# Product keys with 112 candidate sums a head, one-hot comparisons of four tokens, gates moved to the first keys' rows, and offset rows loaded ahead

## The chip, the cores and the metric

The kernel runs on one NeuronCore of one Trainium2 chip. The metric is device time in microseconds, the median of several runs. The engines are named as in the profile: PE (TensorE, matrix products), DVE (VectorE), ACT (ScalarE), POOL (GpSimd) and SP (the queue that issues the weight loads).

## The reference

Two blocks follow each other over 256 tokens of width 1024. The change touches the first block, and one preparation for the second.

First block: a mixer (`h @ w_in`, two branches with sigmoid gates `zg`, two branch products `ab`, `w_out`), then the retrieval of experts by product keys:

```
s = einsum('thpc,hpkc->thpk', q, sub_keys)          # 8 heads, 2 halves, 128 keys
top_s, top_i = top_k(s, 16)
cand_s = top_s[:, :, 0, :, None] + top_s[:, :, 1, None, :]   # 16 x 16 = 256 sums a head
fin_s, fin_pos = top_k(cand_s, 16)
idx = cand_i at fin_pos                             # first key * 128 + second key
gates = softmax(fin_s)
act = gelu(u[idx] . h);  out = sum(gates * act * v[idx])
```

Second block: RWKV and MoBA mixing, then 32 experts with top 4; their weights are the large stream at the end, and their biases ("offsets", `moe_b`) are prepared in the first block.

## The kernel before

Products run in fp32r, in three matrix products for one: each 512-column piece of a weight is cut into a high part (ACT, line 282) and a low part (DVE, line 285; with `cut["aid"]` set, every fourth low part goes to POOL). `gemm` takes one piece for four groups of three 128x256 products (lines 215 to 217) and then calls `tick`, which hands out background work from the list `bg`: each entry has a cost, and `tick` emits entries while a credit (`rate` a tick) lasts. Nothing else sets the order; each engine runs its instructions in the order in which they were written. Weights come as 1 MB tiles through a ring that SP fills when a tile is free.

The stages that matter here, in order:

- `zg`: 8 units of two products each, followed by a sigmoid on ACT into `sg`.
- `ab`: 16 products of 12 matmuls. After products 0, 3 and 6 stands `offset_rows(i)`: a load of 512 columns of `moe_b` into `bf` by POOL's queue (line 501), a copy to `br` on ACT (line 502), two subtractions on POOL (line 504) and a store of `br` to `bd` (line 505). `bf` and `br` have one buffer each.
- `xo`, `qp`: the output product and the queries, with 32 searches for the first 16 of 128 keys (`topk16`, lines 579 to 584) as background work.
- Top-k stage, under the products `up` of the experts' first matrices (64 units of 48 matmuls): for each half of the tokens `cand` on POOL (line 602, four instructions of 128x512, 256 sums a head), eight searches over 256 sums, `place` (the two key positions from the place of a sum: a shift by 4, an AND with 15), `cmp` (comparison with 0 to 15 on DVE, line 646, and a product on POOL, line 649) and `red`.
- Gate stage, under the rest of `up`: for each token a 128x128 one-hot `ah` of the first key on POOL (line 752) and `bh` of the second key times the gate on DVE (line 753), a product `gp` of the two for four tokens (line 764), and `gate_put`, which multiplies the gates into the units that are done and copies them to the others. The loop over `up` leaves the top-k stage at the first unit after `bg` is empty; `credit["rate"]` then spreads the gate work over the units left.
- `vo`, RWKV and MoBA, and the 32 experts (`w<-in_moe_dram`).

Of the kernel before, what the change touches and what calls it, by code (L numbers as in the profile page):

```python
# [35 lines left out]
def tile_model(ctx: ExitStack, tc: tile.TileContext, a, out, taps=None):  # L36
    nc = tc.nc
# [72 lines left out]
    bd = dram.tile([128, 1536], F32R, name="bd")  # L110
# [7 lines left out]
    idx_t = p2.tile([128, 3, T], F32, name="idx_t")  # L118
    iota = p2.tile([128, 128], F32, name="iota")
# [23 lines left out]
    def part(x, k):  # L143
        return x[0][:, k, :], x[1][:, k, :]
# [243 lines left out]
    with ExitStack() as ph:  # L388
# [70 lines left out]
        for j in range(4):  # L459
            zc = psa.tile([128, 2, T], F32, tag="mm", name="zc")  # L460
            zv = psa.tile([128, T], F32, tag="mm", name="zv")
            z_chunk(zc[:, 0, :])
            z_chunk(zc[:, 1, :])
            csb = p1w.tile([128, 2, T], F32, tag="csb", name="csb")
            nc.scalar.copy(csb, zc)
            z_chunk(zv)
            u = p1w.tile([128, 2 + T], F32, tag="cu", name="cu")
            acc = p1w.tile([128, T], F32, tag="cacc", name="cacc")

            def conv_a(j=j, u=u, acc=acc, csb=csb, zv=zv):  # L470
# [12 lines left out]
            later(0.7, split, part(yT, j), acc)  # L483
        sg = p1.tile([128, 2, 8, T], F32, tag="sg", name="sg")
        for b in range(2):
            for m2 in range(4):
# [8 lines left out]
        bsp = ph.enter_context(tc.tile_pool(name="bsp", bufs=1))  # L495

        def offset_rows(i):

            f = bsp.tile([128, 512], F32, tag="bf", name="bf")
            r = bsp.tile([128, 512], F32R, tag="br", name="br")  # L500
            nc.gpsimd.dma_start(f, a["moe_b"][:, i * 512:(i + 1) * 512])
            nc.scalar.copy(r, f)
            for q in (slice(32, 64), slice(96, 128)):
                nc.gpsimd.tensor_tensor(r[q, :], f[q, :], r[q, :].bitcast(F32), op=ALU.subtract)
            nc.gpsimd.dma_start(bd[:, i * 512:(i + 1) * 512], r)

        mT = p1.tile([128, 8, T], F32, name="mT")
        for b, src in ((0, pT), (1, yT)):
            for m in range(8):
                ab = psa.tile([128, T], F32, tag="mm", name="ab")  # L510
                gemm(ab, src, 4, tick)
                if b == 0:
                    nc.vector.tensor_tensor(mT[:, m, :], sg[:, 0, m, :], ab, op=ALU.mult)
                else:
                    t2 = p1w.tile([128, T], F32, tag="t2", name="t2")
                    nc.vector.tensor_tensor(t2, sg[:, 1, m, :], ab, op=ALU.mult)
                    nc.gpsimd.tensor_tensor(mT[:, m, :], mT[:, m, :], t2, op=ALU.add)
                if b == 0 and m in (0, 3, 6):
                    offset_rows(m // 3)

        def m_of(k):
            split(part(hT, k), mT[:, k, :])
# [70 lines left out]
    def topk_of(t):  # L593
        ts, ti = ts2[t], ti2[t]
        tv = ts.rearrange("p (h s) k -> p h s k", s=2)
        big = {}

        def cand(i):
            if i == 0:
                big["c"] = tkw.tile([128, 8, 16, 16], F32, tag="big", name="cand")  # L600
            hh = slice(2 * i, 2 * i + 2)
            nc.gpsimd.tensor_tensor(big["c"][:, hh], tv[:, hh, 0, :, None].to_broadcast([128, 2, 16, 16]),
                                    tv[:, hh, 1, None, :].to_broadcast([128, 2, 16, 16]), op=ALU.add)
        for i in range(2):
            later(0.2, cand, i)
        fs = tkw.tile([128, 8, 16], F32, tag="fs", name="fs")
        fp = tkw.tile([128, 8, 16], U32, tag="fp", name="fp")
        for h in range(8):
            def one(h=h):
                topk16(big["c"][:, h].rearrange("p a b -> p (a b)"), fs[:, h], fp[:, h], 256, "r2")()  # L610
            bg.append((1.8, one))
            if h in (1, 3):
                later(0.2, cand, 2 + h // 2)
        sel = tkw.tile([128, 3, 128], F32, tag="sel", name="sel")

        e = tkw.tile([128, 8, 16], F32, tag="e", name="e")
# [10 lines left out]
                                    sm[:, :, None].to_broadcast([128, 8, 16]), op=ALU.mult)  # L627
        for s in range(2):
            def place(s=s):
                kq = tkw.tile([128, 8, 16], U32, tag="kq", name="kq")  # L630
                if s == 0:
                    nc.vector.tensor_scalar(kq, fp, 4, None, op0=ALU.logical_shift_right)
                else:
                    nc.vector.tensor_scalar(kq, fp, 15, None, op0=ALU.bitwise_and)
                kf = tkw.tile([128, 8, 16], F32, tag="kf", name="kf")
                nc.vector.tensor_copy(kf, kq)
                tf = tkw.tile([128, 8, 16], F32, tag="tf", name="tf")
                nc.vector.tensor_copy(tf, ti.rearrange("p (h s) k -> p h s k", s=2)[:, :, s, :])
                big["k"], big["t"] = kf, tf

            def cmp(i, s=s):
# [5 lines left out]
                                        big["k"][:, hh].rearrange("p h k -> p (h k)")[:, :, None].to_broadcast([128, 32, 16]),  # L647
                                        iota16[:, None, :].to_broadcast([128, 32, 16]), op=ALU.is_equal)
                nc.gpsimd.tensor_tensor(b, b, big["t"][:, hh, None, :].to_broadcast([128, 2, 16, 16]), op=ALU.mult)
            later(0.5, place)  # L650
            for i in range(4):
                later(0.65, cmp, i)

# [90 lines left out]
    hot = {}  # L744

    def one_hot(t0):

        ah = gw_p.tile([128, 2, 128], F32, tag="ah", name="ah", bufs=4)
        bh = gw_p.tile([128, 2, 128], F32, tag="bh", name="bh", bufs=4)
        for i in range(2):  # L750
            t = t0 + i
            nc.gpsimd.tensor_scalar(ah[:, i, :], iota, idx_t[:, 0, t:t + 1], None, op0=ALU.is_equal)  # L752
            nc.vector.tensor_scalar(bh[:, i, :], iota, idx_t[:, 1, t:t + 1], idx_t[:, 2, t:t + 1],
                                    op0=ALU.is_equal, op1=ALU.mult)
        hot[t0] = (ah, bh)

    gps = {}

    def gate_mm(t0):

        gp = psb.tile([128, 4, 128], F32, tag=f"acc{(t0 // 4) % 4}", name="gp")
        for i in range(4):
            ah, bh = hot[t0 + i - i % 2]
            nc.tensor.matmul(gp[:, i, :], ah[:, i % 2, :], bh[:, i % 2, :], start=True, stop=True)  # L764
        gps[t0] = gp

    def gate_put(t0):
# [1314 lines left out]
```

## Time and profile before

| what | before |
|---|---|
| median of 3 runs | 2248.0 us (2244.45 to 2250.05) |
| profiled execution, its own time | 2248.25 us |
| its span in the trace | 2246.4 us |
| PE busy | 2126.2 us, 95% |
| DVE busy | 1185.4 us, 53% |
| ACT busy | 742.3 us, 33% |
| POOL busy | 406.5 us, 18% |

The profiled execution lies 0.25 us above the median, and 1.85 us of it lie outside the span. The busy shares are means over stages: DVE is nearly always busy in the top-k stage and idle most of the time among the 32 experts. "Busy" of PE is modelled from pipelined instructions, so the number of matmuls in a stretch (x in brackets) tells more than the share.

### The profile page before, as it was taken

What the parts mean: (1) busy time and instruction counts of PE and PEld (TensorE: products, weight loads), DVE (VectorE), ACT (ScalarE), POOL (GpSimd) and SP (SyncE); (2) the same over time, 40 slices, a digit from 0 to 9 for tenths busy, and PEclk for the clock granted to TensorE, in tenths of its full rate; (3) what the DMA queues carried; (4) which work ended last, traced back from release to release, by engine and by line L of the source; (5) the groups of instructions that cost most, each with busy time, mean ns of one, the idle gap of its engine ahead of it and who ended that gap; (6) DMA issues with size and microseconds to landing.
All of it is one profiled execution on the core that took longest, in us unless ns stands there. A gap on an engine that the chain in (4) does not pass through costs nothing.

```text
span 2246.4 us, 34028 instructions
## 1 busy us (share of the span) xinstructions
PE 2126.2 (95%) x13130; PEld 1455.9 (65%) x13131; DVE 1185.4 (53%) x2527; ACT 742.3 (33%) x1591; POOL 406.5 (18%) x501
## 2 busy tenths in 40 slices
PE   8989998999999999999999989999999999999897
PEld 8979998999997788887878644333333333333332
DVE  5567998778888888867775522222222122221121
ACT  5545545444435555556553311110000000000000
POOL 3032365766650000001451100000000000000000
PEclk9999999999999999999998989999999999999999
DMA  5555444443336777765321689999999999999998
GB/s 214 191 174 188 170 153 155 144 137 146 132 132 235 288 282 281 284 220 189 119 95 40 256 344 408 420 420 419 420 419 420 420 419 420 419 419 420 420 420 315
DMA packets 90679, 627.07 MB, mean 279 GB/s; under 512 B 10248, under 2 KB 10960, under 8 KB 15760
## 3 DMA queue, kind: packets, MB, share of 16 engines
q1 hardware_dynamic: 88080, 616.68, 69.7%
q0 software_dynamic: 1664, 4.94, 0.6%
q10 hardware_dynamic: 768, 3.21, 0.4%
q8 instruction: 106, 1.74, 0.3%
q14 instruction: 61, 0.50, 0.1%
HBM read 621.86 MB, written 2.93 MB: 278 GB/s over the span
## 4 chain that ended last, share of the span: by engine, by line
PE 52%; DMA 36%; DVE 6%; issue 2%; ACT 2%; POOL 1%; SPq 0%; DVEq 0%; ACTq 0%; POOLq 0%
DMA w<-in_moe_dram 33%; PE vo L215 5%; PE vo L216 5%; PE vo L217 5%; PE up L217 4%; PE up L216 4%; PE up L215 4%; PE pdn L1862 2%; PE gp L764 2%; DVE ws L285 2%; DMA wm<-in_moe_dram 2%; PE pgate L1862 2%; PE pup L1862 2%; PE pgt L1787 1%; PE qp L215 1%
## 5 line engine op out<-in xcount | busy, mean ns | idle before, releaser
L285 DVE TENSOR_TENSOR ws<-w,ws 128x512 fp32r<-128x512 f32 x559 | 402.9, 726 | 148.2 <-ACT ws L282 140.3
L282 ACT CAST ws<-w 128x512 fp32r<-128x512 f32 x581 | 355.5, 623 | 184.3 <-PE vo L217 76.3
L1862 PE MATMUL pup<-w,xe 128*64 128x512 f32 x976 | 246.4, 595 | 30.1 <-DMA w<-in_moe_dram 29.9
L1862 PE MATMUL pgate<-w,xe 128*64 128x512 f32 x968 | 239.4, 597 | 14.1 <-DMA w<-in_moe_dram 13.6
L1862 PE MATMUL pdn<-w,at 128*64 128x512 f32 x968 | 227.2, 596 | 0.3 <-ACT at L1831 0.3
L217 PE MATMUL up<-h2h,ws 128*128 128x256 f32 x676 | 195.5, 289 | 10.3 <-POOL ws L285 6.6
L752 POOL TENSOR_SCALAR ah<-iota,idx_t 128x128 f32<-128x128 f32 x256 | 186.1, 743 | 95.7 <-PE gp L764 95.7
L215 PE MATMUL up<-h2h,ws 128*128 128x256 f32 x676 | 197.1, 292 | 1.7 <-ACT ws L282 1.7
L1862 PEld LDWEIGHTS pup<-w,xe 128*64 128x64 f32 x976 | 76.4, 137 | 186.3 <-issue 125.8
L216 PE MATMUL up<-h2l,ws 128*128 128x256 f32 x676 | 191.9, 284 | 0.0
L215 PE MATMUL vo<-ws,xh 128*128 128x512 f32 x480 | 189.0, 394 | 0.0
L216 PE MATMUL vo<-ws,xh 128*128 128x512 f32 x480 | 188.4, 393 | 0.6 <-DVE ws L285 0.6
L217 PE MATMUL vo<-ws,xl 128*128 128x512 f32 x480 | 187.7, 391 | 0.0
L1862 PEld LDWEIGHTS pgate<-w,xe 128*64 128x64 f32 x968 | 72.3, 137 | 148.8 <-issue 115.0
L1831 ACT COPY at<-pat 128x512 f32<-128x512 f32 x32 | 18.8, 587 | 452.6 <-PE pat L1830 452.6
L1862 PEld LDWEIGHTS pdn<-w,at 128*64 128x64 f32 x968 | 70.6, 137 | 125.4 <-issue 124.0
L1823 DVE TENSOR_SCALAR wm<-pup 128x512 f32<-128x512 f32 x32 | 22.1, 692 | 244.1 <-PE pup L1862 244.1
L1915 DVE TENSOR_TENSOR y<-pdn,gate 128x512 f32<-128x512 f32 (+1 forms) x33 | 22.2, 675 | 229.5 <-PE pdn L1862 229.5
L217 PEld LDWEIGHTS up<-h2h,ws 128*128 128x128 f32 x676 | 130.2, 193 | 15.7 <-DVE ws L285 8.1
L215 PEld LDWEIGHTS up<-h2h,ws 128*128 128x128 f32 x676 | 130.2, 193 | 2.4 <-ACT ws L282 2.3
L216 PEld LDWEIGHTS up<-h2l,ws 128*128 128x128 f32 x676 | 130.4, 193 | 0.0
L1822 ACT ACTIVATE wm<-act 128x512 f32<-128x512 f32 x32 | 20.2, 631 | 333.1 <-DVE act L1821 333.1
(684 smaller groups left out, 4220.4 us busy)
## 6 DMA issues: line engine op xcount, KB each, us to landing
w<-in_moe_dram SPq DMA_DIRECT2D x360, 1024.0 KB, 19.9
w<-in_eu_dram SPq DMA_DIRECT2D x64, 1024.0 KB, 4.8
w<-in_ev_dram SPq DMA_DIRECT2D x64, 1024.0 KB, 5.0
w<-in_w_ada_dram SPq DMA_DIRECT2D x24, 1024.0 KB, 5.5
wm<-in_moe_dram SPq DMA_DIRECT2D x20, 1024.0 KB, 19.9
w<-in_w_mix_dram SPq DMA_DIRECT2D x18, 1024.0 KB, 4.7
w<-in_w_in_dram SPq DMA_DIRECT2D x15, 1024.0 KB, 4.9
w<-in_w_q_dram SPq DMA_DIRECT2D x8, 1024.0 KB, 4.8
```

The lines of the kernel that those rows point to most:

```text
L215: nc.tensor.matmul(dst, lhs[0], rhs[0], start=start, stop=False)
L216: nc.tensor.matmul(dst, lhs[0], rhs[1], start=False, stop=False)
L217: nc.tensor.matmul(dst, lhs[1], rhs[0], start=False, stop=stop)
L282: nc.scalar.copy(h, src)
L285: eng.tensor_tensor(l, src, h.bitcast(F32), op=ALU.subtract)
L752: nc.gpsimd.tensor_scalar(ah[:, i, :], iota, idx_t[:, 0, t:t + 1], None, op0=ALU.is_equal)
L764: nc.tensor.matmul(gp[:, i, :], ah[:, i % 2, :], bh[:, i % 2, :], start=True, stop=True)
L1787: nc.tensor.matmul(p[:, k, :], x_sb[:, t, s], oh[:, t, :], start=(t == 0), stop=(t == 1))
L1822: nc.scalar.activation(sg, act, AF.Sigmoid, scale=1.702)
L1823: nc.vector.tensor_scalar(u, pu, 7.0, -7.0, op0=ALU.min, op1=ALU.max)
L1862: nc.tensor.matmul(p[hs[j], :], lhs[:, 4 * kh + k, hs[j]], g[j][:, k, :], start=False, stop=(kh == 1 and k == 3))
L1915: nc.vector.tensor_tensor(y[:, s], pd[h][:, s.start - 512 * h:s.stop - 512 * h], gate2[:, s], op=ALU.mult)
```

## The change

Four edits.

1. `offset_rows` is split. `offset_load` issues the load of `bf` after the `zg` units 0, 3 and 6; the copy, the subtractions and the store follow after the `zg` units 2 and 5 and, for the third, after product 2 of `ab`.
2. `cand` forms 112 sums a head in place of 256: the first 4 keys of one half with all 16 of the other, and the other 12 with the first 4. It takes two instructions (512 and 384 elements a partition) for all heads in place of four of 512. The eight searches run over 112 values, and the positions in `place` come from new arithmetic: two shifts, two copies and a maximum for the first, two products, a maximum, a copy and a sum for the second. The costs handed to `tick` are 1.1 in place of 1.8 for a search and 1.2 in place of 0.5 for `place`.
3. `bh` becomes one comparison of 128x512 for four tokens (two broadcast tensors) in place of four of 128x128 with the gate as a second operation. It has two buffers of four tokens, where it had four of two.
4. The gate is the second operation of `ah` on POOL.

```
+        def offset_load():
+            f = bsp.tile([128, 512], F32, tag="bf", name="bf")
+            nc.gpsimd.dma_start(f, a["moe_b"][:, len(offs) * 512:(len(offs) + 1) * 512])
+            offs.append(f)
+
+        def offset_rows(i):
+
+            f = offs[i]
+            r = bsp.tile([128, 512], F32R, tag="br", name="br")
+            nc.scalar.copy(r, f)
+            for q in (slice(32, 64), slice(96, 128)):
+                nc.gpsimd.tensor_tensor(r[q, :], f[q, :], r[q, :].bitcast(F32), op=ALU.subtract)
+            nc.gpsimd.dma_start(bd[:, i * 512:(i + 1) * 512], r)
...
+                n = 4 * b + m2
+                if n in (0, 3, 6):
+                    offset_load()
+                elif n in (2, 5):
+                    offset_rows(n // 3)
...
-                if b == 0 and m in (0, 3, 6):
-                    offset_rows(m // 3)
+                if b == 0 and m == 2:
+                    offset_rows(2)
...
             if i == 0:
-                big["c"] = tkw.tile([128, 8, 16, 16], F32, tag="big", name="cand")
-            hh = slice(2 * i, 2 * i + 2)
...
+                big["c"] = tkw.tile([128, 8, 112], F32, tag="big", name="cand")
+            c, (f, l), n = ((big["c"][:, :, 0:64], (0, 4), 16), (big["c"][:, :, 64:112], (4, 16), 4))[i]
...
-            bg.append((1.8, one))
-            if h in (1, 3):
-                later(0.2, cand, 2 + h // 2)
+                topk16(big["c"][:, h], fs[:, h], fp[:, h], 112, "r2")()
+            bg.append((1.1, one))
...
                 if s == 0:
-                    nc.vector.tensor_scalar(kq, fp, 4, None, op0=ALU.logical_shift_right)
+
+                    for dst, by in ((kt, 4), (kf, 2)):
+                        kq = tkw.tile([128, 8, 16], U32, tag="kq", name="kq")
+                        nc.vector.tensor_scalar(kq, fp, by, None, op0=ALU.logical_shift_right)
+                        nc.vector.tensor_copy(dst, kq)
+                    nc.vector.scalar_tensor_tensor(kf, kf, -12.0, kt, op0=ALU.add, op1=ALU.max)
                 else:
-                    nc.vector.tensor_scalar(kq, fp, 15, None, op0=ALU.bitwise_and)
...
+                    i_ = big["k"]
+                    nc.vector.tensor_scalar(kt, i_, -4.0, -48.0, op0=ALU.mult, op1=ALU.add)
+                    nc.vector.scalar_tensor_tensor(kt, i_, -16.0, kt, op0=ALU.mult, op1=ALU.max)
+                    nc.vector.tensor_copy(kf, fp)
+                    nc.vector.tensor_tensor(kf, kf, kt, op=ALU.add)
...
-            later(0.5, place)
+            later(1.2, place)
...
-            nc.gpsimd.tensor_scalar(ah[:, i, :], iota, idx_t[:, 0, t:t + 1], None, op0=ALU.is_equal)
-            nc.vector.tensor_scalar(bh[:, i, :], iota, idx_t[:, 1, t:t + 1], idx_t[:, 2, t:t + 1],
+            nc.gpsimd.tensor_scalar(ah[:, i, :], iota, idx_t[:, 0, t:t + 1], idx_t[:, 2, t:t + 1],
                                     op0=ALU.is_equal, op1=ALU.mult)
-        hot[t0] = (ah, bh)
+        if t0 % 4 == 0:
+            bh = gw_p.tile([128, 4, 128], F32, tag="bh", name="bh")
+            nc.vector.tensor_tensor(bh, iota[:, None, :].to_broadcast([128, 4, 128]),
+                                    idx_t[:, 1, t0:t0 + 4, None].to_broadcast([128, 4, 128]), op=ALU.is_equal)
+            hot["b", t0] = bh
+        hot[t0] = ah
```

The order of instructions moves at these places. On ACT, at the passage from `zg` to `ab`, before (`br<-bf` is the copy in `offset_rows`, `ws<-w` the high part of a weight piece, `sg<-zg` a unit's sigmoid):

```order
L494 ACTIVATE sg<-zg 128x512
L282 CAST ws<-w 128x512 x4
L494 ACTIVATE sg<-zg 128x512
L282 CAST ws<-w 128x512
L502 CAST br<-bf 128x512
L282 CAST ws<-w 128x512 x3
L502 CAST br<-bf 128x512
L282 CAST ws<-w 128x512 x3
L502 CAST br<-bf 128x512
L282 CAST ws<-w 128x512 x9
```

And now, from the third unit of `zg` on:

```order
L511 ACTIVATE sg<-zg 128x512
L496 CAST br<-bf 128x512
L282 CAST ws<-w 128x512 x4
L511 ACTIVATE sg<-zg 128x512
L282 CAST ws<-w 128x512 x4
L511 ACTIVATE sg<-zg 128x512
L282 CAST ws<-w 128x512 x4
L511 ACTIVATE sg<-zg 128x512
L496 CAST br<-bf 128x512
L282 CAST ws<-w 128x512 x4
```

Two of the three copies now stand in `zg`, three units apart; the third stands in `ab`, two pieces later than the first one stood, and no copy follows it. On POOL and SP nothing moves at this place: POOL's order of load, subtractions and store is the same as before.

On DVE in the gate stage, before (`bh` for two tokens or four at a time, `xa<-xa,gp` is `gate_put`, `xb<-xb,tmp` the finished unit's gelu times its gates):

```order
L285 TENSOR_TENSOR ls_1905<-w,hs_1904 128x512
L772 TENSOR_TENSOR xa<-xa,gp 128x4x60
L753 TENSOR_SCALAR bh<-iota,idx_t 128x128 x2
L739 TENSOR_TENSOR xb<-xb,tmp 128x2x40
L285 TENSOR_TENSOR ws<-w,ws 128x512
L753 TENSOR_SCALAR bh<-iota,idx_t 128x128 x2
L285 TENSOR_TENSOR ws<-w,ws 128x512
L772 TENSOR_TENSOR xa<-xa,gp 128x4x60
```

And now:

```order
L285 TENSOR_TENSOR ls_1905<-w,hs_1904 128x512
L775 TENSOR_TENSOR bh<-iota,idx_t 128x512
L759 TENSOR_TENSOR xa<-xa,tmp 128x2x24
L285 TENSOR_TENSOR ws<-w,ws 128x512 x2
L794 TENSOR_TENSOR xa<-xa,gp 128x4x52
L775 TENSOR_TENSOR bh<-iota,idx_t 128x512
L285 TENSOR_TENSOR ws<-w,ws 128x512
L285 TENSOR_TENSOR ls_1905<-w,hs_1904 128x512
L794 TENSOR_TENSOR xa<-xa,gp 128x4x52
```

One `bh` stands where four stood. On PE the first `gp` now follows 1080 matmuls of `up`, where it followed 1224: three units of 48 have moved from the top-k stage into the gate stage. The last `gp` follows 3000 of the 3072 in both.

## Rows read from the trace of the kernel before

**Rows 1.** Page, section 4: the chain that ended last, by engine.

```profile
PE 52%; DMA 36%; DVE 6%; issue 2%; ACT 2%; POOL 1%; SPq 0%; DVEq 0%; ACTq 0%; POOLq 0%
```

**Rows 2.** Windows by stage: zg, ab, top-k twice, RWKV with MoBA, experts.

```profile
core 0: us, PE busy (x) PEld busy (x) DVE busy (x) ACT busy (x) POOL busy (x), PEclk, DMA share, GB/s
63.30:109.40 46.10, 46.10 (x387) 46.10 (x386) 24.46 (x37) 24.80 (x42) 1.80 (x3) 1.00 0.55 192
109.40:145.40 36.00, 27.41 (x194) 26.51 (x193) 20.46 (x31) 12.36 (x24) 19.61 (x18) 0.86 0.46 154
196.00:300.00 104.00, 104.00 (x873) 104.00 (x872) 99.01 (x375) 55.20 (x98) 31.80 (x23) 1.00 0.47 163
300.00:380.00 80.00, 69.03 (x528) 67.38 (x528) 77.06 (x132) 33.29 (x55) 46.13 (x30) 0.94 0.42 145
...
1045.00:1290.00 245.00, 234.04 (x2347) 188.61 (x2345) 156.64 (x285) 116.49 (x250) 78.24 (x88) 0.94 0.35 128
...
1433.00:2213.00 780.00, 724.46 (x3294) 273.77 (x3290) 157.68 (x316) 69.44 (x156) 0.00 (x0) 1.00 1.01 420
```

**Rows 3.** The chain in order of time: start us, us, what.

```profile
95.04 0.12 PE zg L215
...
115.11 5.33 DMA bf<-in_moe_b_dram
...
125.06 6.17 DMA bf<-in_moe_b_dram
...
481.21 0.89 PE gp L764 x8
```

**Rows 4.** Waits, 90 to 200 us: us in total, times, longest.

```profile
ACT br L502 <- DMA bf<-in_moe_b_dram: 14.9, 2, 8.6
PE ab L215 <- ACT ws L282: 7.1, 2, 3.7
```

**Rows 5.** Lines by form, 196 to 388 us, DVE, and one of POOL.

```profile
L285 DVE TENSOR_TENSOR ls<-w,hs 128x512 fp32r<-128x512 f32 x48 | 42.2, 894 | 4.7 <-ACT hs L282 4.7
L583 DVE FIND_INDEX8 ti<-ts,sc 128x8 uint32<-128x128 f32 x32 | 9.1, 286 | 0.0
L583 DVE FIND_INDEX8 fp<-fs,cand 128x8 uint32<-128x256 f32 x16 | 6.7, 420 | 0.0
L632 DVE TENSOR_SCALAR kq<-fp 128x128 uint32<-128x128 uint32 x2 | 0.4, 220 | 0.0
L626 DVE TENSOR_TENSOR sel<-e,sm 128x128 f32<-128x128 f32 x2 | 0.6, 292 | 0.1
L602 POOL TENSOR_TENSOR cand<-ts 128x512 f32<-128x512 f32 x8 | 10.3, 1293 | 0.0
```

**Rows 6.** Lines by form, 388 to 700 us, DVE and POOL.

```profile
L285 DVE TENSOR_TENSOR ws<-w,ws 128x512 fp32r<-128x512 f32 x129 | 88.9, 693 | 31.7 <-ACT ws L282 31.3
L753 DVE TENSOR_SCALAR bh<-iota,idx_t 128x128 f32<-128x128 f32 x256 | 78.5, 356 | 0.1
L752 POOL TENSOR_SCALAR ah<-iota,idx_t 128x128 f32<-128x128 f32 x255 | 185.1, 742 | 95.7 <-PE gp L764 95.7
```

**Rows 7.** Single lines of the source: ns min/median/max, first and last start.

```profile
L752 POOL TENSOR_SCALAR ah<-iota,idx_t x256: 597/607/1800, 386.8 to 668.1; 128x128 f32<-128x128 f32 x128
L764 PE MATMUL gp<-bh,ah x512: 271/275/348, 391.9 to 674.1; 128*128 128x128 f32 x171
L646 DVE TENSOR_TENSOR cmp<-kf,iota x16: 679/1216/1797, 294.8 to 366.2; 128x512 f32<-128x512 f32 x16
```

**Rows 8.** Windows of 24 us in the gate stage; columns as in the first window table.

```profile
404.00:428.00 24.00, 24.00 (x206) 24.00 (x205) 18.36 (x46) 11.61 (x33) 16.45 (x23) 1.00 0.38 132
...
476.00:500.00 24.00, 23.96 (x204) 23.75 (x203) 19.40 (x48) 10.32 (x29) 14.36 (x20) 1.00 0.40 140
...
548.00:572.00 24.00, 23.56 (x192) 22.79 (x191) 20.49 (x48) 9.57 (x28) 14.66 (x20) 1.00 0.38 133
...
644.00:668.00 24.00, 23.14 (x187) 22.20 (x187) 21.12 (x47) 9.21 (x27) 14.88 (x21) 1.00 0.38 136
```

More of the change, by code (lines that the diff above doesn't have):

```diff
@@ L483, in tile_model @@
             later(0.7, split, part(yT, j), acc)
+        bsp = ph.enter_context(tc.tile_pool(name="bsp", bufs=1))
+        offs = []
+        def offset_load():
[9 more added lines that the diff above has]
+            nc.gpsimd.dma_start(bd[:, i * 512:(i + 1) * 512], r)
         sg = p1.tile([128, 2, 8, T], F32, tag="sg", name="sg")
@@ L494, in tile_model @@
                 nc.scalar.activation(sg[:, b, 2 * m2:2 * m2 + 2, :], zg, AF.Sigmoid)
[L495 to L505, printed above, removed]
+                n = 4 * b + m2
[3 more added lines that the diff above has]
+                    offset_rows(n // 3)
         mT = p1.tile([128, 8, T], F32, name="mT")
@@ L599, in cand @@
             if i == 0:
-                big["c"] = tkw.tile([128, 8, 16, 16], F32, tag="big", name="cand")
-            hh = slice(2 * i, 2 * i + 2)
-            nc.gpsimd.tensor_tensor(big["c"][:, hh], tv[:, hh, 0, :, None].to_broadcast([128, 2, 16, 16]),
-                                    tv[:, hh, 1, None, :].to_broadcast([128, 2, 16, 16]), op=ALU.add)
+                big["c"] = tkw.tile([128, 8, 112], F32, tag="big", name="cand")
+            c, (f, l), n = ((big["c"][:, :, 0:64], (0, 4), 16), (big["c"][:, :, 64:112], (4, 16), 4))[i]
+            shape = [128, 8, l - f, n]
+            nc.gpsimd.tensor_tensor(c.rearrange("p h (i j) -> p h i j", j=n), tv[:, :, 0, f:l, None].to_broadcast(shape),
+                                    tv[:, :, 1, None, 0:n].to_broadcast(shape), op=ALU.add)
         for i in range(2):
@@ L609, in one @@
             def one(h=h):
-                topk16(big["c"][:, h].rearrange("p a b -> p (a b)"), fs[:, h], fp[:, h], 256, "r2")()
-            bg.append((1.8, one))
-            if h in (1, 3):
-                later(0.2, cand, 2 + h // 2)
+                topk16(big["c"][:, h], fs[:, h], fp[:, h], 112, "r2")()
+            bg.append((1.1, one))
         sel = tkw.tile([128, 3, 128], F32, tag="sel", name="sel")
@@ L629, in place @@
             def place(s=s):
-                kq = tkw.tile([128, 8, 16], U32, tag="kq", name="kq")
+                kf = tkw.tile([128, 8, 16], F32, tag="kf", name="kf")
+                kt = tkw.tile([128, 8, 16], F32, tag="kt", name="kt", bufs=1)
                 if s == 0:
-                    nc.vector.tensor_scalar(kq, fp, 4, None, op0=ALU.logical_shift_right)
-                else:
-                    nc.vector.tensor_scalar(kq, fp, 15, None, op0=ALU.bitwise_and)
-                kf = tkw.tile([128, 8, 16], F32, tag="kf", name="kf")
-                nc.vector.tensor_copy(kf, kq)
+                    for dst, by in ((kt, 4), (kf, 2)):
[3 more added lines that the diff above has]
+                    nc.vector.scalar_tensor_tensor(kf, kf, -12.0, kt, op0=ALU.add, op1=ALU.max)
+                else:
+                    i_ = big["k"]
[3 more added lines that the diff above has]
+                    nc.vector.tensor_tensor(kf, kf, kt, op=ALU.add)
                 tf = tkw.tile([128, 8, 16], F32, tag="tf", name="tf")
@@ L748, in one_hot @@
         ah = gw_p.tile([128, 2, 128], F32, tag="ah", name="ah", bufs=4)
-        bh = gw_p.tile([128, 2, 128], F32, tag="bh", name="bh", bufs=4)
         for i in range(2):
             t = t0 + i
-            nc.gpsimd.tensor_scalar(ah[:, i, :], iota, idx_t[:, 0, t:t + 1], None, op0=ALU.is_equal)
-            nc.vector.tensor_scalar(bh[:, i, :], iota, idx_t[:, 1, t:t + 1], idx_t[:, 2, t:t + 1],
+            nc.gpsimd.tensor_scalar(ah[:, i, :], iota, idx_t[:, 0, t:t + 1], idx_t[:, 2, t:t + 1],
                                     op0=ALU.is_equal, op1=ALU.mult)
-        hot[t0] = (ah, bh)
+        if t0 % 4 == 0:
[4 more added lines that the diff above has]
+        hot[t0] = ah
     gps = {}
@@ L762, in gate_mm @@
         for i in range(4):
-            ah, bh = hot[t0 + i - i % 2]
-            nc.tensor.matmul(gp[:, i, :], ah[:, i % 2, :], bh[:, i % 2, :], start=True, stop=True)
+            nc.tensor.matmul(gp[:, i, :], hot[t0 + i - i % 2][:, i % 2, :], hot["b", t0][:, i, :], start=True, stop=True)
         gps[t0] = gp
```

## The prediction, made before the changed kernel ran

> **What bounds the kernel now.** I read the chain that ended last first. It is PE for half of the span and DMA for a third [rows 1]. The windows by stage say where: from 1433 us to 2213 us the experts' weights come at 420 GB/s with the DMA engines' share at 1.01, so these 780 us are fixed by bytes. Before them, from 1045 to 1290 us, the share is 0.35 [rows 2]: the stream is waiting for work to be done and for tiles to come free, not the reverse. So whatever the stages ahead of it lose or gain passes on to the end. All four edits lie ahead of 700 us.
>
> In these stages PE is the engine to fill, and the number of matmuls in a window is the measure. A 128x256 matmul starts every 0.12 us where nothing holds it [rows 3]. `zg` runs at this pace, with 387 matmuls in 46.1 us, `ab` with 194 in 36.0 us does not, and its granted clock is 0.86. The top-k stage runs at 873 in 104 us (8.39 a us) up to 300 us and at 528 in 80 us after that, with DVE busy 77 of 80 us [rows 2]. In the gate stage the count falls from 206 in 24 us to 187, while DVE's busy time rises from 18.4 to 21.1 us [rows 8].
>
> **Edit 1, the offset rows.** In `ab` the copy to `br` sits in ACT's queue among the cuts. It waits 14.9 us in two waits for the load of `bf` [rows 4], because each load is issued only when the subtractions before it are done and then takes 5.33 and 6.17 us on the chain [rows 3]. Behind the copy stand the next high parts, and PE waits for those [rows 4]. Without it the 192 matmuls of `ab` take 192 x 0.12 = 23.0 us, against 36.0: 13.0 us, in which the reduced clock after each stop is included.
>
> What takes its place? The load is issued at least two units (2 x 48 x 0.12 = 11.5 us) ahead of its copy. POOL's order is unchanged, so the second load is issued behind the first store; the next copy comes three units, 17.3 us, after the first. The longest load shown is 6.17 us, plus about 4 us of subtractions and issue. `br` has one buffer too, but its store has the same 17 us. The copies in `zg` hide behind ACT's idle half (24.8 of 46.1 us busy [rows 2]); if that cover were gone, a copy and a blocked low part would hold PE for 1 to 2 us each. I take 12.5 us gained (11 to 13).
>
> **Edit 2, the searches.** A search operation takes 0.420 us over 256 values and 0.286 over 128 [rows 5]. The slope gives 0.134 x 144/128 = 0.151 us less for 112. Five operations for 16 searches: 12.1 us of DVE. `place` adds, for each half of the tokens, a shift, a copy and a maximum for the first position, about 0.22 + 0.22 + 0.29 us, and for the second 0.22 + 0.29 + 0.22 + 0.29 in place of 0.22 + 0.22 [rows 5]: 2.6 us for both halves. `cand` on POOL falls from 8 x 1.293 to 2 x 1.293 + 2 x 0.97 = 4.5 us [rows 5], which relieves DVE by 0 to 5.8 us where the two hold each other up; I take 2. DVE has 11.5 us less.
>
> But the costs told to `tick` fall by 16 x 0.7 + 4 x 0.2 - 4 x 0.7 = 9.2 us, at 0.8 a tick 11.5 ticks, and the order shows three units fewer in this stage. PE loses 144 x 0.12 = 17.3 us of work here; DVE loses 9 of 12 low parts, 8.0 us at 0.894 [rows 5], and thus 19.5 us in all. Both shrink together. What PE loses here, 80 x 8.39 - 528 = 143 matmuls or 17.1 us, is DVE's excess in the comparisons, and these stay. I take 2 us gained, with bounds of -4 (the longer `place` meets POOL's products) and +8 (half of the loss). The three units are not saved; they are done later.
>
> **Edits 3 and 4, the gate stage.** It lasts from 391.9 us to 674.1 plus one matmul [rows 7], 282.5 us. Its work is 1776 matmuls of `up` at 0.12 and 512 records of `gp` at 0.89 / 8 [rows 3]: 270.1 us. So 12.4 us are lost. The windows with DVE at 18.4 us lose nothing, those with 20.5 and 21.1 lose 14 and 19 matmuls of 206 [rows 8], so I put the loss down to DVE's queue, in which a low part stands behind `bh` and `gate_put`.
>
> `bh` holds DVE 78.5 us in 256 instructions [rows 6]. The new form is not in the trace. The nearest row from below is a low part beside the same `ah`, also two tensors of 512 from SBUF: 0.693 us [rows 6]; from above it is `cmp`, the same operation and broadcasts beside longer POOL products: 0.679 at least, 1.216 in the median [rows 7]. I take 0.693, since the neighbour is the same `ah`: 64 x 0.693 = 44 us, 34 less, or 2.9 in each 24 us. The late windows come down to 17.6 to 18.2 us, where nothing is lost. I take 9 of the 12.4 us (4 to 12), as the last units before `vo` have other waits.
>
> `ah` with a second operation is not in the trace either. It takes 0.607 us in the median and 0.742 in the mean, and POOL waits 95.7 us for PE to give back its buffers [rows 6, 7]. The second operation is free at best; at worst it is a second pass, 0.742 + 0.607 = 1.35 us. With 1920 matmuls of `up` the stage now needs 287.4 us for 63 groups of four tokens, so `ah` costs nothing below 287.4 / 252 = 1.14 us. I take about 0.80. The Trainium skill (GPSIMD Engine Reference, section "Elementwise — side-by-side cycle accounting") says that one or two operations an element are bound by the ports alike; by that it would stay at 0.742, and no run here shows it yet.
>
> **Sum.** 12.5 + 2 + 9 = 23.5 us. The profiled execution took 2248.25, its span and 1.85 us around it, and lies 0.25 above the median: 2248.25 - 23.5 = 2224.75, so **2225 us**.
>
> **The rivals.**
>
> *`bh` doesn't get cheaper.* At 1.216 us 64 of them take 78 us, as long as the 256 before. Then 0.5 us or so is left of edit 3: 2248.25 - 12.5 - 2 - 0.5 = 2233. For it speaks that `cmp` is the same instruction; against it, that the low parts beside `ah` stay at 0.693.
>
> *POOL and DVE exclude each other.* If an instruction of either that reads two, or any, tensors from SBUF shut the other out for its whole length, four tokens would need 4 x 0.607 on POOL, 0.693 for `bh` and 2.54 low parts at 0.693: 4.88 us, or 307 us for the stage. That is 20 us of loss for 12.4: 2248.25 - 14.5 + 7.6 = 2241. The Trainium skill states such a lock (SBUF — State Buffer, section "Who interferes with whom"). The rows do not bear it out at this length: by the same sum the stage before would have needed 2.43 + 4 x 0.356 + 2.35 x 0.693 = 5.48 us a group, and it took 282.5 / 63 = 4.48.
>
> *The offset wait only moves.* If each copy in `zg` stopped PE for 3 us, 9 of the 13 us would come back: 2234. ACT's idle half speaks against it.
>
> *`ah` becomes the bound, and the kernel gets slower.* Above 1.14 us POOL sets the pace of the gate stage; above 1.27 us the loss (252 x 1.27 = 320, 33 us over 287) has eaten all three gains and 6 us more. At 1.35 us the stage takes 340 us: 2248.25 - 14.5 + 52.6 - 12.4 = 2274. POOL's waits for PE speak against it.
>
> *The gains are absorbed.* If the experts' stream were bound by the time at which its loads could start, none of this would show: about 2247. The share of 0.35 ahead of it speaks against that.
>
> **How the numbers follow.** A difference of 0.3%, 6.7 us, is what a measurement of this kernel can tell. My forecast (2216 to 2233) gets 0.60, the dear `bh` 0.15, the moved wait 0.09, the exclusion 0.05, absorption 0.05, the dear `ah` 0.06. Faster: 0.60 + 0.15 + 0.09 + 0.03 of the exclusion = 0.87; same 0.07; slower 0.06. The range 2213 to 2238 takes in the forecast, with both bounds of the searches, the dear `bh` and the moved wait, and leaves out the other 0.16.
>
> **What would show it.** `ab` should take 23 to 25 us with no wait of ACT for `bf` and a clock of 1.00. The first `gp` should come 30 to 34 us earlier (12.5 + 2 + 17.3). The search operations should take about 0.27 us. In the gate stage `bh` should be near 0.69 us, `ah` below 1 us with POOL still waiting for PE, and the late windows should hold 200 matmuls or more in 24 us. The step before the experts' stream and the stream itself should keep their lengths. I would be wrong if `bh` or `ah` take twice as long, or if PE waits more for low parts that POOL cuts among the comparisons.

## The result and the profile after

The changed kernel takes 2214.9 us in the median of 4 runs (2212.47 to 2217.86), beside 2247.8 (2244.45 to 2250.05) for the kernel before: a ratio of 0.9861, with a 95% interval of 0.9848 to 0.9873. It is faster by 32.9 us, where 23.5 were forecast; 2225 was predicted. The time lies inside the range of 2213 to 2238, and 1.1 us below the band of 2216 to 2233 that the forecast gave itself. The profiled execution, the fastest of the four, took 2212.47 us; its span is 2210.7 us, 35.7 less than before.

The chain that ended last, from the page of the kernel after:

```profile
PE 64%; DMA 30%; DVE 3%; ACT 1%; issue 1%; POOL 0%; SPq 0%; DVEq 0%; ACTq 0%; POOLq 0%
```

PE's share was 52% and DVE's 6% [rows 1]: the chain runs less over DVE, ACT and POOL (4%, where it was 9%). The shares move by far more than 35.7 us, so they tell where the chain runs and not how much was gained. Windows of the kernel after, by stage: `zg`, `ab`, the top-k stage twice, the gate stage twice, one late piece of it as long as those of [rows 8], and the RWKV projections:

```profile
core 0: us, PE busy (x) PEld busy (x) DVE busy (x) ACT busy (x) POOL busy (x), PEclk, DMA share, GB/s
62.90:110.00 47.10, 47.03 (x386) 46.22 (x385) 27.43 (x38) 25.67 (x44) 9.89 (x11) 1.00 0.61 203
110.00:132.80 22.80, 22.80 (x195) 22.80 (x194) 18.17 (x32) 11.57 (x21) 10.91 (x10) 1.00 0.62 211
184.00:272.00 88.00, 88.00 (x739) 88.00 (x738) 82.92 (x369) 46.98 (x84) 22.41 (x17) 1.00 0.48 169
272.00:344.00 72.00, 64.64 (x513) 63.22 (x513) 71.02 (x135) 30.87 (x53) 45.76 (x29) 0.98 0.42 149
356.00:500.00 144.00, 144.00 (x1222) 144.00 (x1221) 100.08 (x180) 74.09 (x192) 142.58 (x129) 1.00 0.43 150
500.00:643.40 143.40, 143.40 (x1217) 143.40 (x1216) 116.11 (x195) 66.04 (x183) 133.81 (x123) 1.00 0.42 146
...
616.00:640.00 24.00, 24.00 (x206) 24.00 (x205) 20.13 (x34) 10.04 (x28) 23.28 (x20) 1.00 0.38 136
...
1017.70:1080.10 62.40, 58.97 (x408) 49.88 (x409) 44.53 (x71) 40.38 (x79) 29.79 (x34) 1.00 0.37 128
```

`ab` does its 192 matmuls without a gap and at the full clock, in 22.8 us for 36.0 [rows 2]. The gate stage has no gap either, and POOL is busy in 142.58 of the first 144 us of it. The late piece holds 206 matmuls, where the last one of [rows 8] held 187, although DVE is busy 20.13 of 24 us in it. In the top-k stage PE's gaps remain in its second half.

Waits of the kernel after, 90 to 200 us and then 356 to 643 us (total us, times, longest):

```profile
POOL br L498 <- ACT br L496: 23.8, 2, 13.4
...
ACT ws L282 <- PE ab L216: 9.3, 13, 0.8
...
POOL ah L771 <- PE gp L786: 9.2, 12, 1.4
```

In place of ACT's 14.9 us for `bf` [rows 4], POOL waits for ACT's copies, and PE waits for nothing behind them in `ab`. ACT now waits for PE there. POOL's waits for PE in the gate stage have gone from 95.7 us [rows 6] to 9.2.

Single lines of the kernel after (ns min/median/max, first and last start):

```profile
L771 POOL TENSOR_SCALAR ah<-iota,idx_t x256: 787/951/2356, 349.6 to 641.0; 128x128 f32<-128x128 f32 x128
L775 DVE TENSOR_TENSOR bh<-iota,idx_t x64: 670/684/826, 353.1 to 639.8; 128x512 f32<-128x512 f32 x64
L786 PE MATMUL gp<-bh,ah x512: 272/275/275, 356.0 to 643.1; 128*128 128x128 f32 x171
```

The first `gp` starts 35.9 us earlier than in [rows 7], the last one 31.0. With PE's first matmul of each stage as marks, the 35.7 us come out as follows; a minus is time gained. Three units of `up` (17.3 us) have moved from the third line to the fourth, so the last column leaves them out.

| stretch | before, us | after, us | difference | without the three units |
|---|---|---|---|---|
| up to the start of `ab` | 109.3 | 110.1 | +0.8 | +0.8 |
| `ab` | 35.9 | 22.8 | -13.1 | -13.1 |
| start of `up` to first `gp` | 165.0 | 141.3 | -23.7 | -6.4 |
| gate stage | 282.5 | 287.4 | +4.9 | -12.4 |
| last `gp` to `vo` | 11.9 | 9.8 | -2.1 | -2.1 |
| all the rest | | | -2.5 | -2.5 |

Most of the last line is one stretch: the RWKV projections between two marks took 64.3 us before and 62.4 after, at a granted clock of 0.95 and 1.00. The change doesn't touch them.

Lines by form of the kernel after, 184 to 352 us (busy us, mean ns | idle before):

```profile
L593 DVE FIND_INDEX8 fp<-fs,cand 128x8 uint32<-128x112 f32 x16 | 4.3, 269 | 0.0
L666 DVE TENSOR_TENSOR cmp<-kf,iota 128x512 f32<-128x512 f32 x16 | 20.4, 1297 | 0.0
...
L615 POOL TENSOR_TENSOR cand<-ts 128x512 f32<-128x512 f32 x2 | 2.6, 1306 | 0.0
L615 POOL TENSOR_TENSOR cand<-ts 128x384 f32<-128x384 f32 x2 | 2.1, 1068 | 0.0
```

A search operation takes 0.269 us (about 0.27 was taken), `cand` 4.7 us in all (4.5 was taken).

### The profile page after: what moved, and what is told of

It is laid out like the page before. It is cut to its first block, busy times and chain, and to the rows that moved or that the text cites. A ratio compares the mean times of both kernels' runs of the same rounds, so it can differ in the third digit from the quotient of the medians.

```text
span 2210.7 us, 33675 instructions
## 1 busy us (share of the span) xinstructions
PE 2108.5 (95%) x13130; PEld 1445.7 (65%) x13131; DVE 1148.2 (52%) x2347; ACT 748.9 (34%) x1597; POOL 493.2 (22%) x494
## 4 chain that ended last, share of the span: by engine, by line
PE 64%; DMA 30%; DVE 3%; ACT 1%; issue 1%; POOL 0%; SPq 0%; DVEq 0%; ACTq 0%; POOLq 0%
DMA w<-in_moe_dram 28%; PE up L217 5%; PE vo L215 5%; PE vo L216 5%; PE up L215 5%; PE up L216 5%; PE vo L217 5%; PE pdn L1884 3%; PE pgate L1884 3%; PE pup L1884 3%; PE gp L786 3%; DMA wm<-in_moe_dram 2%; PE pgt L1809 1%; DVE ws L285 1%; PE pout L1859 1%
## 5 line engine op out<-in xcount | busy, mean ns | idle before, releaser
L282 ACT CAST ws<-w 128x512 fp32r<-128x512 f32 x584 | 361.0, 621 | 203.0 <-PE vo L217 76.3
L771 POOL TENSOR_SCALAR ah<-iota,idx_t 128x128 f32<-128x128 f32 x256 | 282.8, 1118 | 9.5 <-PE gp L786 9.2
L1884 PE MATMUL pgate<-w,xe 128*64 128x512 f32 x968 | 239.8, 599 | 12.9 <-DMA w<-in_moe_dram 12.3
```

The lines of the kernel that those rows point to most:

```text
L282: nc.scalar.copy(h, src)
L1884: nc.tensor.matmul(p[hs[j], :], lhs[:, 4 * kh + k, hs[j]], g[j][:, k, :], start=False, stop=(kh == 1 and k == 3))
```

## The experiments

In this part "loss" is the length of the gate stage (last `gp` start less first, plus 0.3 us) less PE's work in it: 0.12 us a matmul of `up`, 0.89 us for each eight records of `gp`, as in the prediction. It was 12.4 us before, and it is 0.0 after.

### One edit at a time

**The offset rows alone** (kernel before with edit 1; the diff is the one shown with the change).

> The kernel before with edit 1 alone (offset rows loaded ahead, their copies in zg). If the waits of ab are simply gone and everything behind moves up: 12 us less than before (11 to 13), ab in 23 us, zg about 1 us longer because POOL's subtractions hold a low part up, the top-k and the gate stage as long as before. If the 33 us came from something that all edits share, or if the time is given back in a later stage: 0 to 5 us less.

Measured: 2231.7 us, ratio 0.9938 (0.9916 to 0.9959), 14 us. Windows of this kernel, `zg` and `ab`:

```profile
63.50:110.00 46.50, 46.42 (x381) 45.61 (x380) 27.42 (x37) 25.16 (x44) 9.89 (x11) 1.00 0.59 199
110.50:133.30 22.80, 22.80 (x193) 22.58 (x191) 18.31 (x32) 11.88 (x22) 11.41 (x10) 1.00 0.64 218
```

`ab` is as short as after, and `up` starts 12.3 us earlier. By PE's first matmuls, 62.9 us in `zg` and 110.1 in `ab`, `zg` is 1.1 us longer than before: the weight loads of PE wait 0.9 us there for low parts, which take 0.82 us in the mean in `zg` for 0.71 before, now that POOL's subtractions run there. The gate stage keeps its loss of 12.3 us, so the two places have nothing to do with each other.

**The keys alone** (kernel before with edit 2, costs included).

> The kernel before with edit 2 alone (112 sums, new places, new costs). If the searches and the smaller cand on POOL are what shortened the top-k stage: 5 to 7 us less than before, with three units of up moved into the gate stage and the loss among the comparisons down from 143 matmuls to about 90. If the three units only move and bring DVE's load with them: 0 to 2 us less.

Measured: 2235.8 us, 0.9955 (0.9938 to 0.9971), 10 us, more than either expectation. From the start of `up` to the first `gp` it takes 140.4 us, so that with the three units added, 157.7 for 165.0, 7.3 are gained. And the gate stage, in which nothing is edited, loses 4.6 us for 12.4. The old `bh` is in this kernel; the relief comes from the three units that moved in.

**The gates alone** (kernel before with edits 3 and 4).

> The kernel before with edits 3 and 4 alone (bh for four tokens, gate on ah). ah took 1.118 us in the changed kernel, and 252 of them are 282 us. Here the gate stage keeps its 1776 matmuls of up, 270 us of PE work. Theory that POOL is at its bound: the stage stays at 280 to 284 us, PE waits on POOL's ah or POOL on nothing, and the kernel gains only 0 to 4 us. Rival, that POOL follows PE and its ah are long only because it has the time: the stage takes 270 to 273 us and the kernel gains 11 to 15 us.

Measured: 2234.3 us, 0.9951 (0.993 to 0.9973), 11 us, at the lower end of the rival's gain; the stage, 274.6 us, lies between the two. The loss is 4.5 us. `ah` of this kernel as a single line of the source:

```profile
L751 POOL TENSOR_SCALAR ah<-iota,idx_t x256: 784/874/2288, 386.4 to 664.9; 128x128 f32<-128x128 f32 x128
```

What PE and its weight loads (PEld) wait for in the stage:

```profile
PEld gp L766 <- POOL ah L751: 3.9, 7, 1.0
...
PE gp L766 <- POOL ah L751: 2.5, 7, 0.8
```

In the kernel before, the weight loads waited for DVE's low parts (388 to 674 us):

```profile
PEld up L217 <- DVE ws L285: 6.1, 18, 0.5
...
PEld up L217 <- DVE ls L285: 1.1, 3, 0.4
```

Of these 7.2 us nothing is left with the new gates.

Two of its windows of 24 us:

```profile
476.00:500.00 24.00, 23.69 (x201) 23.50 (x200) 16.76 (x32) 12.18 (x31) 24.00 (x23) 1.00 0.39 134
...
636.00:660.00 24.00, 24.00 (x206) 24.00 (x205) 21.19 (x35) 9.76 (x28) 24.00 (x21) 1.00 0.43 159
```

POOL is busy in 24.00 of 24 us in both, and `ah` is all that PE waits for: with 270.1 us of PE's work POOL is the bound, and the stage takes 274.6. The first of the two windows loses 5 matmuls of 206 with DVE at 16.76 us; late in the stage, at 21.19 us of DVE, all 206 go through. So the wait that the prediction named, for low parts in DVE's queue, is gone, but the busy time of DVE, by which it measured the cause, doesn't decide the loss.

### What in the keys gains

**Edit 2 with the old costs.**

```
-            bg.append((1.1, one))
+            bg.append((1.8, one))
-            later(1.2, place)
+            later(0.5, place)
```

> Edit 2 alone, but with the old costs told to tick (1.8 for a search, 0.5 for place). The first gp then follows 1176 matmuls of up, not 1080. If DVE's shorter work is what counts: 6 to 10 us less than before, as DVE has the same work less and two more units to spread it over. If the pacing was the gain (fewer units in a stage that DVE bounds, more in the next): 0 to 3 us less.

Measured: 2238.1 us, 0.9967 (0.9956 to 0.9978). The gate stage starts after 1176 matmuls of `up`, one unit less than before and not three; 4.0 us are gained ahead of it, and the loss is 8.8 us. The time lies in the range for DVE's shorter work.

**The new costs alone** (kernel before, only the two numbers changed).

> The kernel before with nothing but the new costs told to tick (1.1 for a search, 1.2 for place); all instructions are those of before, three units of up move from the top-k into the gate stage. If the thinner spread alone relieves the gate stage: its loss falls from 12.4 to 4 to 6 us, as in the run with the keys alone. DVE's searches, not shortened, then press on fewer ticks: the first gp comes only 8 to 10 us earlier for 17.3 us of PE work less. In all -2 to +3 us against before. If the pacing were the whole gain of edit 2: 8 to 10 us less than before.

Measured: 2243.8 us, 0.9989 (0.9979 to 1.0). The first `gp` comes 10.0 us earlier, with 17.3 us less of PE's work ahead of it: 7.3 us more are lost in the top-k stage. The gate stage loses 5.0 us for 12.4, 7.4 less. So the numbers by themselves trade one loss for the other.

The difference between this kernel and the keys alone is that of the searches, `place` and `cand` at the same pace: -7.3 against +7.3, 14.6 us. Added up by line, DVE's instructions in the stretch take 13.7 us less: 12.1 less in the searches, 5.5 less in the low parts (0.78 us in the mean for 0.87), 2.8 more in `place` and 1.2 more in `cmp`. In the new costs alone five of the six low parts between 259 and 274 us, where `cand` and POOL's own low parts run, take 1.1 to 1.8 us; the sixth takes 0.67.

**More work for POOL beside `cand`** (kernel after, with four sums of 128x512 that nobody reads).

```
+            d = tkw.tile([128, 2, 16, 16], F32, tag="dummy", name="dummy", bufs=1)
+            nc.gpsimd.tensor_tensor(d, tv[:, 0:2, 0, :, None].to_broadcast([128, 2, 16, 16]),
+                                    tv[:, 0:2, 1, None, :].to_broadcast([128, 2, 16, 16]), op=ALU.add)
```

> The changed kernel with four more sums of 128x512 on POOL beside cand (into a tile that nobody reads), so that POOL has 5.2 us more there, as it had before. If the smaller cand is part of the gain in the top-k stage, because POOL and DVE hold each other up: the first gp comes 1.5 to 4 us later. If the searches and the pacing alone are: less than 1 us.

Measured, in one run: 2221.2 us. The first `gp` comes 5.3 us later, more than either expectation, for the 4.7 us that the four sums took. But PE loses nothing where the sums of the first half stand. Two windows of this run, and then the second of them for the kernel after, which had the same 739 matmuls from 184 to 272 us:

```profile
184.00:272.00 88.00, 88.00 (x739) 88.00 (x739) 83.02 (x362) 47.00 (x84) 24.93 (x18) 1.00 0.48 169
272.00:300.00 28.00, 22.78 (x167) 21.38 (x166) 27.86 (x32) 10.01 (x17) 21.96 (x15) 0.95 0.33 116
```

```profile
272.00:300.00 28.00, 23.99 (x183) 23.38 (x183) 27.86 (x36) 11.34 (x20) 21.57 (x15) 0.94 0.41 150
```

No instruction of DVE waits for `cand` or for the added sums. Beside them its low parts get longer (from 246 to 270 us `ls` takes 0.97 us in the mean and `ws` 0.86, in the kernel after 0.77 and 0.68), the first comparison starts 2.1 us later, and PE's matmuls are missing among the comparisons. So POOL's time reaches PE through DVE's queue; why 4.7 us there become 5.3 was not followed further.

**No low parts on POOL among the comparisons** (kernel after).

```
             def place(s=s):
+                if s == 0:
+                    cut["aid"] = False
...
         def red(s, i):
+            if s == 1 and i == 1:
+                cut["aid"] = True
```

> The changed kernel with the low parts kept on DVE while comparisons are pending (POOL takes every fourth as before in the rest of the top-k stage). Some seven low parts move from POOL, at 1.5 to 1.7 us each, to DVE at 0.69. If POOL's time counts one for one among the comparisons, as the run with more sums showed: the first gp comes 3 to 6 us earlier than in the changed kernel, PE no longer waits for POOL's low parts, and the kernel is 3 to 6 us faster. If the loss there is DVE's load alone: 2 to 5 us slower.

Measured: 2212.6 us, 0.9846 (0.983 to 0.9861), the same as after. POOL's busy time from 272 to 344 us fell from 45.8 to 33.7, but `up` to first `gp` is only 0.4 us shorter, and neither the gain of 3 to 6 us nor the loss of 2 to 5 came. PE's waits in the top-k stage, of the kernel after and then of this one:

```profile
PE up L217 <- POOL ws L285: 4.5, 2, 3.0
...
PE up L217 <- DVE ws L285: 2.0, 3, 1.0
...
PE up L217 <- DVE ls L285: 0.8, 1, 0.8
```

```profile
PE up L217 <- DVE ws L285: 5.0, 3, 2.7
...
PE up L217 <- DVE ls L285: 2.1, 1, 2.1
```

The wait for POOL has become a wait for DVE of about the same size (7.3 and 7.1 us in all).

### The gate stage

**`ah` with one operation.** The gate is left out here, so the weights of the experts are missing from the sums.

```
-            nc.gpsimd.tensor_scalar(ah[:, i, :], iota, idx_t[:, 0, t:t + 1], idx_t[:, 2, t:t + 1],
-                                    op0=ALU.is_equal, op1=ALU.mult)
+            nc.gpsimd.tensor_scalar(ah[:, i, :], iota, idx_t[:, 0, t:t + 1], None, op0=ALU.is_equal)
```

> The changed kernel with the gate left out of ah, so that the experts' outputs are not weighted; every other instruction stands as in the changed kernel. If the second operation is what lengthened ah: its minimum falls from 0.787 to 0.60 us, its mean from 1.118 to 0.80 to 0.90, and POOL waits 40 us or more for PE again. If the longer bh on DVE did it: the mean stays above 1.0. Time: 0 to 3 us less than the changed kernel if POOL does not hold PE up there, as its trace says; 5 or more if it does after all.

Measured: 2213.6 us, 0.9856 (0.9833 to 0.9878), the same as after; the stage takes 287.3 us. Its `ah`, by form:

```profile
L771 POOL TENSOR_SCALAR ah<-iota,idx_t 128x128 f32<-128x128 f32 x255 | 193.7, 776 | 94.7 <-PE gp L785 93.4 <-ACT ws L282 1.0
```

One operation takes 0.776 us in the mean beside the new `bh`, two take 1.118. The 0.34 us of difference are all taken out of POOL's waits for PE, and none reaches the time.

**`bh` as four instructions** (kernel after).

```
-            nc.vector.tensor_tensor(bh, iota[:, None, :].to_broadcast([128, 4, 128]),
-                                    idx_t[:, 1, t0:t0 + 4, None].to_broadcast([128, 4, 128]), op=ALU.is_equal)
+            for i in range(4):
+                nc.vector.tensor_scalar(bh[:, i, :], iota, idx_t[:, 1, t0 + i:t0 + i + 1], None, op0=ALU.is_equal)
```

> The changed kernel with bh as four comparisons of 128x128 again (without the gate, which stays on ah). If DVE's time for bh is what held the low parts up: DVE is 30 us longer busy in the gate stage, the loss there comes back to 3 to 6 us, and the kernel takes 2 to 6 us more than the changed one. If the gate stage is at full rate only because three more units of up are spread over it: no difference within 1.5 us.

Measured: 2216.3 us, 0.9862 (0.9839 to 0.9885), the same as after. The stage takes 287.3 us, with no loss, though `bh` holds DVE 59.1 us in place of 44.3 (14.8 us more, where 30 were expected). The late window of this kernel, and then one of the keys alone, which has the old gates at the same spread:

```profile
616.00:640.00 24.00, 24.00 (x205) 24.00 (x204) 20.94 (x48) 10.00 (x28) 22.97 (x20) 1.00 0.42 150
```

```profile
604.00:628.00 24.00, 23.66 (x196) 23.06 (x195) 20.82 (x47) 9.77 (x29) 15.23 (x21) 1.00 0.38 132
```

DVE is as busy in the one as in the other, and busier than in the piece of [rows 8] that lost 14 matmuls; the old gates lose 10 here, the new ones none. Once the gate has left `bh` and the work is spread over three units more, the one instruction for four is not needed.

**A fifth one-hot on POOL** (kernel after; the fifth isn't read).

```
+        if t0 % 4 == 2:
+            ax = gw_p.tile([128, 128], F32, tag="ax", name="ax", bufs=1)
+            nc.gpsimd.tensor_scalar(ax, iota, idx_t[:, 0, t0:t0 + 1], idx_t[:, 2, t0:t0 + 1],
+                                    op0=ALU.is_equal, op1=ALU.mult)
```

> The changed kernel with a fifth one-hot of the same form for every four tokens on POOL, which nobody reads. At 1.118 us each the five would take 63 x 5.6 = 352 us, at the least duration seen (0.787) 248 us, and PE has 287 us of work. If POOL is at its bound and its instructions have a time of their own: the gate stage takes 300 to 350 us and the kernel 12 to 60 us longer. If they only fill the time that PE leaves them: 287 to 292 us, and the same time.

Measured, in one run: 2253.3 us, more than the kernel before, which took 2246.4 in the median on the same chip. The stage takes 324.6 us, 37.2 over PE's work. Its waits:

```profile
PE gp L790 <- POOL ah L771: 21.6, 43, 0.8
```

A quarter more work for POOL costs all that the change gains. That is the rival in which `ah` becomes the bound, and it was near: in the gates alone POOL's 256 `ah` took 276.6 us with POOL never waiting for long, against the 287.4 us that the stage lasts after. By that run some 4% are in hand.

**A slower pace in the comparisons** (kernel after, the cost of `cmp` 1.1 for 0.65), and **the same with every fourth `ah` on DVE**.

```
-                later(0.65, cmp, i)
+                later(1.1, cmp, i)
...
+            eng = nc.vector if t % 4 == 3 else nc.gpsimd
+            eng.tensor_scalar(ah[:, i, :], iota, idx_t[:, 0, t:t + 1], idx_t[:, 2, t:t + 1],
```

> The changed kernel with the cost of a comparison told to tick raised from 0.65 to 1.1, which moves two units of up back into the top-k stage (first gp after 1176). If the loss among the comparisons is DVE's and POOL's excess over the credit: it falls from 91 matmuls (11 us) to 40 or fewer, and the first gp comes 4 to 8 us earlier than the two units (11.5 us) later. The gate stage then has 276 us of PE work, and if POOL is near its bound there, as in the run with the gates alone, it loses 3 to 6 us. In all -4 to +2 us against the changed kernel. If POOL is not near its bound: -5 to -8 us.

> As the run with slow comparisons, and every fourth ah on DVE, which takes a quarter of the load from POOL and gives DVE about 64 x 0.34 = 22 us. If POOL's bound is what eats the gain of the slow comparisons: 3 to 6 us less than in that run, and 4 to 8 us less than the changed kernel. If DVE's load is what counts in the gate stage: the same as in that run, or up to 4 us more.

Measured: 2213.2 us, 0.9854 (0.983 to 0.9878), and 2215.0 us, 0.9854 (0.9832 to 0.9877). Two units move back into the top-k stage, which then loses 3.3 us less (4 to 8 were expected). The gate stage, now with 275.8 us of work, loses 1.7 us (3 to 6) with POOL at the bound. With a quarter of `ah` on DVE POOL has 73.6 us of waits for PE again, and the loss is still 1.5 us, though the windows of 24 us from 366 to 630 us hold 205 or 206 matmuls each; the one wait of PE in the stage comes after them, 0.9 us of `gp` for `bh` on DVE. So POOL isn't alone in what is lost at the denser spread, and the gain of 3 to 6 us over the run before did not come. Neither time can be told from that of the change.

### The gate stage in all runs

| kernel | PE's work, us | length, us | loss, us |
|---|---|---|---|
| before | 270.1 | 282.5 | 12.4 |
| offset rows alone | 270.1 | 282.4 | 12.3 |
| gates alone | 270.1 | 274.6 | 4.5 |
| keys, old costs | 275.8 | 284.6 | 8.8 |
| after, slower comparisons | 275.8 | 277.5 | 1.7 |
| after, the same and `ah` partly on DVE | 275.8 | 277.3 | 1.5 |
| new costs alone | 287.4 | 292.4 | 5.0 |
| keys alone | 287.4 | 292.0 | 4.6 |
| after | 287.4 | 287.4 | 0.0 |
| after, more work beside `cand` | 287.4 | 287.4 | 0.0 |
| after, no low parts on POOL | 287.4 | 287.4 | 0.0 |
| after, `ah` with one operation | 287.4 | 287.3 | 0.0 |
| after, `bh` in four | 287.4 | 287.3 | 0.0 |
| after, a fifth one-hot | 287.4 | 324.6 | 37.2 |

With the old gates the loss falls from 12.4 to 8.8 to about 5 us as the work grows from 270 to 287 us; with the new ones it is 8 us less at 270 and nothing is left to lose at 287.

## Why the prediction was right, and where its sizes were off

**The offset rows: right.** 12.5 us were taken. 13.1 are gained in `ab` and 0.8 are paid ahead of it, 12.3 net. The wait did not move, the clock of `ab` is 1.00, and no wait for `bf` is left on ACT.

**The searches: right in kind, too small.** 2 us were taken, 6.4 came (7.3 alone). The working was sound: DVE, busy 95% of the time, bounds this stretch, and at equal pace its work falls by 13.7 us and the stretch by 14.6. The searches came as costed (12.1), and `place` nearly (2.8 for 2.6). The mis-sized term is the relief by `cand`, of which 2 of 5.8 us were counted; the low parts took 5.5 less. With 5.8 the prediction's own sum, 12.1 - 2.6 + 5.8 + 8.0 - 17.3, gives 6.0 us. The run with more work beside `cand` bears out that POOL and DVE hold each other up there.

**"The three units are not saved; they are done later": true, but half of the price was left out.** In the top-k stage the prediction did price the move, with 17.3 us of PE's work against 8.0 of low parts, 9.3 us; the new costs alone show 7.3. What it left out is the other side: in the gate stage the same move gives 7.4 us back. The two cancel in that run, but not in the changed kernel, where the new gates alone already bring the loss down to 4.5.

**The gate stage: the size nearly right, the wait right, its measure wrong.** 9 of 12.4 us were taken, all 12.4 came, the upper bound. The wait that was named, for a low part in DVE's queue, is what goes: 7.2 us of weight loads before, none in the gates alone or after. The step that failed is the one that read the size of the cause out of the windows of [rows 8]: those with 20.5 and 21.1 us lose, so fewer microseconds of DVE. `bh` fell as predicted, from 78.5 to 44.3 us at 0.684 us in the median (0.693 was taken). But the late windows still have DVE at 20.1 us, not 17.6 to 18.2, and lose nothing; the gates alone pass 206 matmuls at 21.19, and `bh` in four instructions 205 at 20.94. DVE's busy time and PE's loss rose together over the stage, but at the same busy time the old gates lose and the new ones don't. What the runs show is that two things each recover nearly 8 us, the wider spread (7.4 to 7.8) and the new gates (7.9), and that together they recover 12.4. The new gates take all of the wait for low parts away, and the 4.5 us that are left when they stand alone are a loss of another kind, at POOL's `ah`. What in the new gates does it stays open: the gate's operation that left `bh`, the cut of its buffers (two of four tokens for four of two), and the order in DVE's queue were not separated. That the upper bound was reached owes something to the spread, which the prediction had not counted here.

**`ah`: mis-sized, at no cost.** 0.80 us was taken, 1.118 is the mean; the least time rose from 0.597 to 0.787 us and the rest came from longer instances. The bound of 1.14 us held, since 252 x 1.118 = 282 us still fit in 287.4. The value lies between the two ends that were given, 0.742 and 1.35, and nearer the middle than the free end that was followed. The Trainium skill (GPSIMD Engine Reference, section "Elementwise — side-by-side cycle accounting") says that with one or two operations an element the ports are the bound; by that the least time should not have moved, and here it rose by 0.19 us, so the measurement decides against it for this instruction.

**The rivals.** The dear `bh` did not come. In the gate stage POOL and DVE do not exclude each other for whole instructions: 4 x 0.787 on POOL, 0.684 for `bh` and 160 / 63 = 2.54 low parts at 0.71 would need 5.6 us a group, and the stage took 287.4 / 63 = 4.56. This is the better test: the sum of 5.48 in the prediction counts `bh` with one tensor, and with instructions of two tensors alone (2.43 + 2.35 x 0.693 = 4.06) it would have fitted the 4.48 before. Beside POOL's products of 128x512 it is otherwise: `cmp` on DVE took 0.679 us at least and 1.758 in the median in the kernel after, so there the two do hold each other up, and whether whole instructions are shut out was not tried. The gains were not absorbed: PE's first matmul of `plog`, just ahead of the experts, comes 35.7 us earlier, and the last one of the experts 35.6.

**Not foreseen at all:** 2.1 us between the last `gp` and `vo`, and about 2 us of clock in the RWKV projections. The first come with the new gates: the stretch takes 9.3 us in the gates alone, and 11.9 to 12.0 in the five kernels with the old gates. The projections vary from 62.3 to 66.2 us among these runs, at a granted clock of 1.00 to 0.92, with edits that have nothing to do with them, and are no gain of the change.

The parts alone gave 14, 10 and 11 us by their ratios, 35 in all, and together they give 31; by their medians it is 32 and 33. The intervals are too wide to call a difference shown, but the stage marks show the overlap: 7.8 + 7.9 us in the gate stage, of which only 12.4 were to be had.

## What to carry to other kernels

When a stage loses a few per cent while an engine beside PE grows busier, test that engine's load as the cause before costing an edit by it, and read what PE waits for: here windows with the same load lost 10 matmuls or none. An engine's instructions can also get longer because another one works, and the loss can show later: here some 20 us after the added sums. A number that paces background work is worth a run of its own, because it moves loss between stages, and a gain by pace and a gain by cheaper work may be the same microseconds. Before giving an idle engine more, work out how long it may be busy before it is the bound; the change left some 4% of that here, and a quarter more work lost everything.

## What the runs showed of the hardware that was not expected

- A second operation in POOL's 128x128 `tensor_scalar` raised its least time from 0.592 us (one operation, beside the same `bh`) to 0.787, and its mean from 0.776 to 1.118.
- `FIND_INDEX8` takes 0.269 us over 112 values, 0.286 over 128 and 0.420 over 256 [rows 5].
- DVE's comparisons of 128x512 took different times beside different work of POOL: `bh` took 0.684 us in the median and 0.826 at most beside `ah`, `cmp` 1.758 and 1.784 beside products of 128x512, at the same least time (0.670 and 0.679), all in the kernel after.
- The same stretch of the RWKV projections had a granted clock between 0.92 and 1.00 from kernel to kernel, though its work was the same; what sets it was not tried.
